# Second FFN layer as seven products of quarters, with operand sums on GpSimd

## The chip, the core and the metric

One Trainium2 chip, one core. The metric is the device time of one execution in microseconds (us); less is better. TensorE (PE) multiplies, VectorE (DVE), ScalarE (ACT) and GpSimd (POOL) work on tiles of 128 partitions, SyncE (SP) and two of the others issue DMAs. A tile of 128x512 float32 has 256 KB.

## What is computed

A trunk layer on 1024 latent rows and 128 prompt rows, 1152 in all, of width 1024. The change is in its last part, the FFN, and the final norm:

```python
h2 = rmsnorm(x, p['norm2_g']) * (1 + sc2) + sh2
a, b = jnp.split(h2 @ p['ffn_w1'], 2, axis=-1)
x = x + g2 * ((jax.nn.silu(a) * b) @ p['ffn_w2'])
...
y_prompt = rmsnorm(xp, final_norm_g)
y_sample = rmsnorm(xs, final_norm_g)
```

`ffn_w2` has 2816 rows, 22 tiles of 128, and 1024 columns. `sc2`, `sh2` and `g2` are one set for the latent rows and one for the prompt's. All is float32.

## The kernel before

A float32 product is made as three fast matmuls. Each operand is split into a high half (a cast on ScalarE) and a low half (source minus high, on VectorE), and `mm3` (L257 to L259) adds high x high, high x low and low x high in PSUM.

The first FFN layer (L1364 to L1366) runs over 22 pairs of weight tiles, one of `a` and one of `b`, on all 1152 rows. A pair is already made as seven products instead of eight: the weights' sums are made on GpSimd (`w_sum`, tile `ws`), three products ahead (`LEAD = 3`) of their matmuls, and split into `wf`. The pair's results go through `evac` into `st`, and `store` splits them into `hl` and writes both halves to DRAM (`hid_d`) from ScalarE's queue. Pair 0 is made apart, in four pieces, since the rows of `h2` come one by one.

The second layer runs in three passes over the inner dimension (tiles 0 to 5, 6 to 13, 14 to 21). In a pass, each of nine row tiles `i` takes its tile `hid` from DRAM and makes two halves of columns, each a chain of three matmuls per inner tile, `f<-w,hid` 128x512. The weights come as `w2r` and are split into `w` (`load_hl`, L1127 and L1128). After each half, VectorE multiplies the sum by the gate row `g2r` (L1570), and GpSimd adds it to `acc` (L1572), which holds `x`; in the last pass VectorE adds (L1574) and ScalarE squares (L1575), VectorE makes the mean (L1578, L1579), GpSimd the power (L280), VectorE the scaled result (L1584), and SP writes it out.

A scheduler sets the order of the instructions of each engine from the order of the code; each engine works its own list in order.

Of the kernel before, what the change touches and what calls it, by code (L numbers as in the profile page):

```python
# [84 lines left out]
def kernel(ctx: ExitStack, tc: tile.TileContext, A: dict, O: dict):  # L85
# [1252 lines left out]
    hid_d = [dp.tile([2, NT, P, b - a, P], F32, name=f"hid{a}_d") for a, b in PASSES]  # L1338

    def stages():  # L1340
        ts_ = [M("st", [P, 2, NCH, HALF]) for _ in range(2)]
        return [t[:, i] for t in ts_ for i in range(2)] + [M("st", [P, NCH, HALF])]
# [155 lines left out]
    def w2_place(j):  # L1498
        if j < 4 or 14 <= j < 18:
            t = zt("w2", [P, 2, D], 4, F32R)  # L1500
            return t[:, 0], t[:, 1]
        if 6 <= j < 12 or j == 21:
            i, n = divmod(j - 6, 3) if j < 12 else (0, 0)
            if n == 0:
                z[i] = wide["right"].tile([P, 3, 2, D], F32R, tag=f"xb{i}", name=nm("w2"), bufs=1)
            return z[i][:, n, 0], z[i][:, n, 1]
        return tuple(slot("w2", dt=F32R) for _ in range(2))

    def w2_load(j):
        if j in w2:  # L1510
            return
        w2[j] = load_hl(zt("w2r", [P, D], 4), *w2_place(j), A["w_ffn2"][j])

    def hid_load(n, i):
        if n == len(PASSES) or (n, i) in hid:
            return
        a, b = PASSES[n]
        t = zt("hid", [P, 2, 8, P], 3, F32R)
        for q in range(2):
            dma(f(t[:, q, :b - a]), hid_d[n][q, i])  # L1520
        hid[n, i] = t[:, 0], t[:, 1]

    order = [(j, i) for j in range(1, NF) for i in range(7)]
    pairs = {}
    for n, (j, i) in enumerate(order):
# [8 lines left out]
        if (j, i) == (NF - 1, 3):  # L1534
            xctx.__exit__(None, None, None)
            open_z()
            for i2 in range(6):
                if i2 < 3:
                    hid_load(0, i2)
                w2_load(i2)  # L1540
# [2 lines left out]
    g2rows, acc = [], []
    for n, (a, b) in enumerate(PASSES):
        for j in range(a, b):
            w2_load(j)
        for i in range(NT):
            for d in range(3):
                hid_load(n + (i + d) // NT, (i + d) % NT)
            h = hid.pop((n, i))  # L1550
            pts = [bank("f2", "m") for _ in range(2)]
            for j in range(a, b):
                for hf in range(2):
                    hs = slice(hf * 512, hf * 512 + 512)
                    last["f2"] = mm3(pts[hf], (h[0][:, j - a], h[1][:, j - a]), (w2[j][0][:, hs], w2[j][1][:, hs]), j == a, j == b - 1)
            if n == i == 0:
                for cnd in range(2):
                    g2rows.append(slot("g2r"))
                    bcast_row(g2rows[cnd], cnd, 5)
                fng = slot("fng")  # L1560
                dma(fng, A["final_g"].partition_broadcast(P))
            if n == 0:
                for i2 in ((0, 1) if i == 0 else (i + 1,) if i + 1 < NT else ()):
                    acc.append(M("acc", [P, D]) if i2 < 8 else slot("acc"))
                    nc.gpsimd.dma_start(acc[i2], x1_d[i2])
            st = small("nst", [P, 3])
            for hf in range(2):
                hs = slice(hf * 512, hf * 512 + 512)
                t = half_slot("fin")
                V.tensor_mul(t, pts[hf], g2rows[i == 8][:, hs])  # L1570
                if n < len(PASSES) - 1:
                    G.tensor_add(acc[i][:, hs], acc[i][:, hs], t)  # L1572
                else:
                    V.tensor_add(acc[i][:, hs], acc[i][:, hs], t)  # L1574
                    S.activation(t, acc[i][:, hs], AF.Square, accum_out=st[:, hf:hf + 1])  # L1575
            if n < len(PASSES) - 1:
                continue
# [165 lines left out]
```

## Time and profile before

| | us |
|---|---|
| median of 3 runs | 2148.88 (2144.29 to 2150.33) |
| the profiled execution | 2148.07 |
| its span, first to last instruction | 2145.9 |
| first layer after pair 0 | 1383.35 to 1856.6 |
| second layer, first to last start of a matmul | 1856.61 to 2137.03 |

The span lies within the execution; 2.2 us are around it. Of a row of the timeline, the bracket says how long the engine had stood idle, and what ended that. In groups by line, "xN | a, b" is the count, the busy time in us and the mean of one in ns.

### The profile page before, as it was taken

To read this page: it belongs to the slowest core of one execution; us is meant where nothing else is said; L and a number is where in the kernel's file an instruction comes from. 1 tells how busy PE (TensorE), PEld (TensorE's weight loads), DVE (VectorE), ACT (ScalarE), POOL (GpSimd) and SP (SyncE) were. 2 spreads that over 40 slices of the span, in tenths; PEclk is the share of its full clock that TensorE was granted. 3 is DMA by queue.
4 is the path that set the end of the run, shared out by engine and by line. 5 is a ranking of instruction groups with operands and counts; after the bars stand their busy time and mean duration, and the time that the engine had idled before them with its cause. 6 is when DMAs were issued, how large, how long until landed. Compare 5 with 4: busy or idle time off the path is not lost.

```text
span 2145.9 us, 31575 instructions
## 1 busy us (share of the span) xinstructions
PE 2070.2 (96%) x12400; PEld 1844.4 (86%) x12400; DVE 1158.8 (54%) x2123; ACT 727.2 (34%) x1320; POOL 406.5 (19%) x344
## 2 busy tenths in 40 slices
PE   6899999999999999999999998899999999999998
PEld 1558888998887799999999876799999999878886
DVE  4733499825443278998823266645445454432134
ACT  3734443445432533332223244423223232310011
POOL 1310020000001202232211234421221212042210
PEclk9999999999999999999999999899999999999999
DMA  8784552233242352242221342222423324764232
GB/s 289 219 278 142 190 185 97 66 105 129 75 146 83 120 193 89 95 133 67 88 69 58 128 157 108 91 84 84 126 84 111 99 88 122 255 236 151 84 137 88
DMA packets 174824, 276.20 MB, mean 129 GB/s; under 512 B 14834, under 2 KB 123987, under 8 KB 174548
## 3 DMA queue, kind: packets, MB, share of 16 engines
q1 hardware_dynamic: 120692, 238.80, 32.9%
q10 hardware_dynamic: 51392, 25.96, 4.4%
q0 software_dynamic: 2592, 9.44, 1.1%
q8 instruction: 97, 1.59, 0.3%
q14 instruction: 51, 0.42, 0.1%
HBM read 196.58 MB, written 77.56 MB: 128 GB/s over the span
## 4 chain that ended last, share of the span: by engine, by line
PE 86%; DVE 5%; DMA 4%; ACT 2%; issue 1%; SPq 1%; POOL 1%; ACTq 0%; DVEq 0%; POOLq 0%
PE gm L257 9%; PE gm L259 9%; PE gm L258 9%; PE f L1365 8%; PE f L1366 8%; PE f L1364 7%; PE f L259 4%; PE f L258 4%; PE f L257 4%; PE po L682 2%; PE ptr L672 2%; PE po L258 1%; PE po L259 1%; PE po L257 1%; PE wo L258 1%
## 5 line engine op out<-in xcount | busy, mean ns | idle before, releaser
L259 PE MATMUL gm<-hT_hi,wlo 128*128 128x384 f32 x1224 | 420.0, 343 | 2.7 <-DVE wlo L233 2.7
L257 PE MATMUL gm<-hT_hi,whi 128*128 128x384 f32 x1224 | 421.6, 344 | 0.7 <-ACT whi L232 0.4
L258 PE MATMUL gm<-hT_lo,whi 128*128 128x384 f32 x1224 | 417.3, 341 | 0.0
L259 PEld LDWEIGHTS gm<-hT_hi,wlo 128*128 128x128 f32 x1224 | 231.1, 189 | 11.5 <-issue 5.1
L257 PEld LDWEIGHTS gm<-hT_hi,whi 128*128 128x128 f32 x1224 | 231.0, 189 | 11.6 <-issue 7.5
L258 PEld LDWEIGHTS gm<-hT_lo,whi 128*128 128x128 f32 x1224 | 231.0, 189 | 5.7 <-issue 3.8
L1364 PE MATMUL f<-xa_hi,wf 128*128 128x288 f32 (+2 forms) x704 | 210.3, 301 | 9.2 <-ACT wf L1334 8.7
L1365 PE MATMUL f<-xa_lo,wf 128*128 128x288 f32 (+2 forms) x704 | 212.6, 303 | 2.1 <-DVE xa_lo L1301 1.9
L1366 PE MATMUL f<-xa_hi,wf 128*128 128x288 f32 (+2 forms) x704 | 210.9, 302 | 0.4 <-DVE wf L1335 0.4
L1173 POOL TENSOR_TENSOR mg<-mg,sg 128x384 f32<-128x384 f32 x72 | 97.3, 1352 | 364.8 <-DVE sg L1169 360.5
L257 PE MATMUL f<-w,hid 128*128 128x512 f32 x396 | 154.7, 394 | 4.2 <-DVE st L1388 2.1
L1365 PE MATMUL f<-xb,wf 128*128 128x288 f32 (+2 forms) x528 | 156.6, 297 | 0.6 <-DVE xb L1301 0.6
L1364 PE MATMUL f<-xb,wf 128*128 128x288 f32 (+2 forms) x528 | 156.9, 297 | 0.0
L1366 PE MATMUL f<-xb,wf 128*128 128x288 f32 (+2 forms) x528 | 156.4, 296 | 0.0
L258 PE MATMUL f<-w,hid 128*128 128x512 f32 x396 | 155.9, 394 | 0.2 <-DVE w L1128 0.2
L259 PE MATMUL f<-w,hid 128*128 128x512 f32 x396 | 155.3, 393 | 0.4 <-DMA hid<-hid_d 0.4
L1364 PEld LDWEIGHTS f<-xa_hi,wf 128*128 128x128 f32 x704 | 135.8, 194 | 10.9 <-ACT wf L1334 9.8
L1168 ACT ACTIVATE sg<-gm,vec 128x384 f32<-128x384 f32 x96 | 55.9, 582 | 243.0 <-PE gm L259 233.6
L1365 PEld LDWEIGHTS f<-xa_lo,wf 128*128 128x128 f32 x704 | 135.0, 192 | 3.7 <-DVE xa_lo L1301 3.4
L1366 PEld LDWEIGHTS f<-xa_hi,wf 128*128 128x128 f32 x704 | 134.5, 192 | 1.3 <-DVE wf L1335 1.2
L1570 DVE TENSOR_TENSOR fin<-f,g2r 128x512 f32<-128x512 f32 x54 | 37.1, 690 | 156.0 <-PE f L259 152.9
L1169 DVE SCALAR_TENSOR_TENSOR sg<-sg,po 128x384 f32<-128x384 f32 x96 | 52.6, 548 | 123.8 <-PE po L259 118.6
(359 smaller groups left out, 4196.7 us busy)
## 6 DMA issues: line engine op xcount, KB each, us to landing
hid_d<-hl ACTq DMA_DIRECT2D x44, 576.0 KB
adaw<-in_ada_w_dram SPq DMA_DIRECT2D x48, 512.0 KB
wraw<-in_w_ffn_dram SPq DMA_DIRECT2D x44, 512.0 KB
wraw<-in_w_gate_dram SPq DMA_DIRECT2D x32, 640.0 KB
hid<-hid_d SPq DMA_DIRECT2D x36, 512.0 KB
wraw<-in_w_o_dram SPq DMA_DIRECT2D x24, 512.0 KB
w2r<-in_w_ffn_dram SPq DMA_DIRECT2D x22, 512.0 KB
wraw<-in_w_in_dram SPq DMA_DIRECT2D x19, 512.0 KB
```

The costliest lines, as they stand in the source:

```text
L257: mm(out, ah, bh, start=start, stop=False)
L258: mm(out, ah, bl, start=False, stop=False)
L259: return mm(out, al, bh, start=False, stop=stop)
L672: tr(pt[:, k * P:(k + 1) * P], pe[:, (k0 + k) * P:(k0 + k + 1) * P], ident)
L682: mm(po[64 * j:64 * j + 64, :P], vtile(kt)[:, h * 64:(h + 1) * 64], pT[:, i, :], start=(i == 0), stop=(i == len(kts) - 1))
L1168: S.activation(sg, pg, AF.Tanh, bias=vc("gate_b", b * 8 + j), scale=0.5)
L1169: V.scalar_tensor_tensor(sg, sg, 1.0, po, op0=ALU.add, op1=ALU.mult)
L1173: G.tensor_add(merged[j][:, cs], merged[j][:, cs], sg)
L1364: mm(out, w[:, 0, ks], x[0], start=st, stop=False, skip_group_check=True)
L1365: mm(out, w[:, 0, ks], x[1], start=False, stop=False, skip_group_check=True)
L1366: mm(out, w[:, 1, ks], x[0], start=False, stop=sp_, skip_group_check=True)
L1570: V.tensor_mul(t, pts[hf], g2rows[i == 8][:, hs])
```

## The change

With the latent rows in two halves of 512 (four row tiles each), the inner dimension in two halves of 11 tiles (`KH`) and the columns in two halves of 512, the second layer becomes a product of 2x2 by 2x2 blocks, made as seven products of sums of blocks instead of eight of blocks. The prompt's 128 rows stay plain products, which are put into products 0, 4, 5 and 6, where a plain block of weights is at hand.

- `store` writes the pair's results unsplit: the prompt's part to `ask_d`, and, once both pairs `jj` and `jj + 11` are there, the blocks A11, A12, A22 and the sums S1 to S4, made on GpSimd (L1408), to `rows_d`. GpSimd issues these DMAs (L1397, L1400). The first layer's pairs run 0, 11, 1, 12 and so on.
- Each of 7 x 11 steps (product `n`, inner tile `jj`) is prepared three steps ahead: a load of rows `ar` (L1547) and of weights `br` (L1511) on SP, in products 1, 2, 3 and 5 a subtraction of weights on GpSimd (L1525, L1529, L1533), and the splits `ah` and `bh` (L1515 on ScalarE, L1516 on VectorE). In product 5 a further split `bx` serves the prompt.
- A step is 4 row tiles x 3 matmuls, and 3 more for the prompt in products 0, 4 and 5; in product 6 the prompt's stand after all steps in the code.
- `evacuate` copies and adds the PSUM sums into four tiles for each block of the result (`c11` and so on); gate, residual, squares and the multiplication by the norm's weights are made block by block.

```diff
-        def store(self):
-            hl = [M("hl", [P, NCH, 2, HALF], F32R) for _ in range(2)]
...
+            put("A11", a11)
+            put("A12", a12)
+            put("A22", a22)
...
+            for o, t, x, y, op in (("S1", s1, a21, a22, G.tensor_add), ("S2", s2, s1, a11, G.tensor_sub),
+                                   ("S3", s3, a11, a21, G.tensor_sub), ("S4", s4, a12, s2, G.tensor_sub)):
+                op(t, x, y)
+                put(o, t)
...
-    order = [(j, i) for j in range(1, NF) for i in range(7)]
+    def weights(jj):
+
+        b = w2_load(0, 0, jj)
+        yield b, None
+        for kh, nh in ((0, 1), (1, 1)):
+            x = w2_load(kh, nh, jj)
+            G.tensor_sub(x, x, b)
+            b = x
+            yield b, None
+        b21, x = w2_load(1, 0, jj), zt("br", [P, 512], 16)
+        G.tensor_sub(x, b21, b)
+        yield x, None
+        yield b21, None
+        b22, b12, x = w2_load(1, 1, jj), w2_load(0, 1, jj), zt("br", [P, 512], 16)
+        G.tensor_sub(x, b22, b12)
+        yield x, b12
+        yield b22, None
...
+        at = zt("ah", [P, 2, 512], 4, F32R)
+        ar = zt("ar", [P, 512], 4)
+        dma(ar, rows_d[SECOND[n], jj])
+        bt = zt("bh", [P, 2, 512], 4, F32R) if n < 6 or jj < 4 else slot("bh", [P, 2, 512], F32R)
+        ready[n, jj] = parts(at, ar), parts(bt, raw)
...
+    def residual(i, h, c):
...
+        V.tensor_mul(c, c, g2rows[i == 8][:, h * 512:h * 512 + 512])
+        G.tensor_add(c, c, x1)
...
+        residual(i, 0, c)
+        squares(i, 0, c)
+        G.tensor_mul(c, c, fng[:, :512])
+
+    def last_product(i, c, ps):
+        t = half_slot("lp")
+        V.tensor_mul(t, ps, g2rows[i == 8][:, 512:])
+        G.tensor_add(c, c, t)
+
+    def finish(i, c0, c1):
+
+        squares(i, 1, c1)
...
+        pow_mhalf(st[:, 3:4], st[:, 2:3])
...
+        V.scalar_tensor_tensor(c1, c1, st[:, 3:4], fng[:, 512:], op0=ALU.mult, op1=ALU.mult)
...
+        elif n == 2:
+            V.tensor_add(a["c21"], a["c11"], ps)
+            G.tensor_add(a["c12"], a["c12"], a["c21"])
...
+        elif n == 5:
+            V.tensor_add(a["c21"], a["c21"], ps)
+            V.tensor_add(a["c22"], a["c12"], ps)
+            residual(q, 1, a["c12"])
+            first_half(4 + q, a["c21"])
+            residual(4 + q, 1, a["c22"])
+            finish(4 + q, a["c21"], a["c22"])
+        else:
+            last_product(q, a["c12"], ps)
+            finish(q, a["c11"], a["c12"])
```

Up to the first rows of pair 0's results, every engine's list is the same as before. ScalarE at the end of pair 0, before: `st` is pair 0's result, `hl` its split, `wf` the split of the next pair's weights, `f` a PSUM bank.

```order
L1374 COPY st_12242<-f_2258_12479 128x192
L1378 ACTIVATE st_12243<-f_2258_12479 128x192
L1385 ACTIVATE st_12242<-st_12242 128x192
L1395 CAST hl_12577<-st_12244 128x3x192
L1395 CAST hl_12577<-st_12243 128x3x192
L1399 DMA hid_d<-hl_12577 128x9x128
L1399 DMA hid_d<-hl_12578 128x9x128
L1334 CAST wf_12589<-wraw_12585 128x512
L1374 COPY st_12613<-f_2275_12616 128x2x3x96
```

The same place of ScalarE after (`hid` takes the place of two of the `st`):

```order
L1376 COPY st_12318<-f_2258_12555 128x192
L1334 CAST wf_12665<-ws_12663 128x512
L1334 CAST wf_12668<-wraw_12654 128x512
L1334 CAST wf_12679<-ws_12661 128x512
L1334 CAST wf_12713<-ws_12711 128x512
L1380 ACTIVATE hid_12320<-f_2258_12555 128x192
L1334 CAST wf_12744<-ws_12742 128x512
L1334 CAST wf_12772<-wraw_12655 128x512
L1387 ACTIVATE st_12318<-st_12318 128x192
L1376 COPY st_12682<-f_2273_12685 128x2x3x96
```

The next pair's first cast (`wf_12589`) stood behind the `hl` rows and the DMAs; now that pair's casts stand between pair 0's rows (its first, `wf_12658`, 34 rows ahead of the first one shown).

VectorE before, for one row tile of the last pass, between its last matmul and its output (`fin` is the gated sum, `nst` the norm's small tile):

```order
L1570 TENSOR_TENSOR fin_18996<-f_2937_18945,g2r_17426 128x512
L1570 TENSOR_TENSOR fin_19000<-f_2938_18946,g2r_17426 128x512
L1574 TENSOR_TENSOR acc_17734<-acc_17734,fin_18996 128x512
L1574 TENSOR_TENSOR acc_17734<-acc_17734,fin_19000 128x512
L1578 TENSOR_TENSOR nst_18995<-nst_18995 128x1
L1579 TENSOR_SCALAR nst_18995<-nst_18995 128x1
L1584 SCALAR_TENSOR_TENSOR acc_17734<-acc_17734,nst_18995,fng_17430 128x512 x2
```

VectorE after, part of what stands between product 5's sums and the split of the rows of step (6,4), `ah_19327` (`c` a block of the result, `rows` the tile with the gate rows and the prompt's result):

```order
L1516 TENSOR_TENSOR ah_19307<-ar_19308,ah_19307 128x512
L1516 TENSOR_TENSOR bh_19310<-br_18881,bh_19310 128x512
L1603 TENSOR_TENSOR c_2817_18006<-c_2817_18006,rows_17442 128x512
L1603 TENSOR_TENSOR rows_17442<-rows_17442 128x512
L1603 TENSOR_TENSOR c_2767_17740<-c_2767_17740,rows_17442 128x512
L1603 TENSOR_TENSOR c_2988_18866<-c_2988_18866,rows_17442 128x512
L1516 TENSOR_TENSOR bh_19430<-br_19073,bh_19430 128x512
L1603 TENSOR_TENSOR c_2818_18007<-c_2818_18007,rows_17442 128x512
L1603 TENSOR_TENSOR c_2768_17741<-c_2768_17741,rows_17442 128x512
L1603 TENSOR_TENSOR c_2989_18867<-c_2989_18867,rows_17442 128x512
L1603 TENSOR_TENSOR c_2818_18007<-c_2818_18007,rows_17442 128x512
L1516 TENSOR_TENSOR ah_19327<-ar_19328,ah_19327 128x512
```

GpSimd at the same place, after (`x` the rows to which the gated sum is added):

```order
L1604 TENSOR_TENSOR c_2817_18006<-c_2817_18006,x_2990_18868 128x512
L1604 TENSOR_TENSOR c_2767_17740<-c_2767_17740,x_3064_19208 128x512
L1615 TENSOR_TENSOR c_2817_18006<-c_2817_18006,rows_17442 128x512
L1604 TENSOR_TENSOR c_2988_18866<-c_2988_18866,x_2990_18868 128x512
L1604 TENSOR_TENSOR c_2817_18006<-c_2817_18006,x_2991_18870 128x512
L1604 TENSOR_TENSOR c_2988_18866<-c_2988_18866,x_2991_18870 128x512
L1604 TENSOR_TENSOR c_2767_17740<-c_2767_17740,x_3068_19231 128x512
L1615 TENSOR_TENSOR c_2817_18006<-c_2817_18006,rows_17442 128x512
L1604 TENSOR_TENSOR c_2818_18007<-c_2818_18007,x_2992_18872 128x512
L1604 TENSOR_TENSOR c_2989_18867<-c_2989_18867,x_2992_18872 128x512
```

Each multiplication by the gate row on VectorE is followed by an addition on GpSimd, and four row tiles of the lower half pass here in full; 24 rows of VectorE run from the first sum of product 5 (L1651) to `ah_19327`, 12 of them shown.

## Rows read from the trace of the kernel before

**Rows 1.** The page: the span, and the chain that ended last by engine.

```profile
span 2145.9 us, 31575 instructions
...
PE 86%; DVE 5%; DMA 4%; ACT 2%; issue 1%; SPq 1%; POOL 1%; ACTq 0%; DVEq 0%; POOLq 0%
```

**Rows 2.** Groups by line and form of the stretch 1856 to 2146 us, the second layer: line, engine, operation, tiles and shapes, count | busy us, mean ns | idle us before them and what ended it.

```profile
L258 PE MATMUL f<-w,hid 128*128 128x512 f32 x396 | 155.9, 394 | 0.2 <-DVE w L1128 0.2
L259 PE MATMUL f<-w,hid 128*128 128x512 f32 x396 | 155.3, 393 | 0.4 <-DMA hid<-hid_d 0.4
L257 PE MATMUL f<-w,hid 128*128 128x512 f32 x396 | 154.7, 394 | 4.2 <-DVE st L1388 2.1 <-DMA hid<-hid_d 2.1
...
L1572 POOL TENSOR_TENSOR acc<-acc,fin 128x512 f32<-128x512 f32 x36 | 50.3, 1421 | 110.6 <-DVE fin L1570 110.6
...
L1584 DVE SCALAR_TENSOR_TENSOR acc<-acc,nst,fng 128x512 f32<-128x512 f32 x18 | 12.7, 749 | 6.3 <-POOL nst L280 6.3
```

**Rows 3.** Timeline of TensorE at the beginning and the end of the second layer: start us, us, engine, line, operation, tiles, shapes, count, [idle before <- what ended it].

```profile
1856.61 0.39 PE L257 MATMUL f<-w,hid 128*128 128x512 f32 x1
1857.19 0.50 PE L258 MATMUL f<-w,hid 128*128 128x512 f32 x1 [0.19 <-DVE w L1128]
...
1860.03 0.50 PE L257 MATMUL f<-w,hid 128*128 128x512 f32 x1 [2.10 <-DVE st L1388]
...
2137.03 0.40 PE L259 MATMUL f<-w,hid 128*128 128x512 f32 x1
```

**Rows 4.** Timelines of VectorE, GpSimd and SP at the end, same columns.

```profile
2136.76 1.39 DVE L1570 TENSOR_TENSOR fin<-f,g2r 128x512 f32<-128x512 f32 x2 [5.05 <-PE f L259]
2138.07 1.28 DVE L1574 TENSOR_TENSOR acc<-acc,fin 128x512 f32<-128x512 f32 x2
2140.29 0.16 DVE L1578 TENSOR_TENSOR nst<-nst 128x1 f32<-128x1 f32 x1 [0.94 <-ACT fin L1575]
2140.48 0.15 DVE L1579 TENSOR_SCALAR nst<-nst 128x1 f32<-128x1 f32 x1
2141.36 1.41 DVE L1584 SCALAR_TENSOR_TENSOR acc<-acc,nst,fng 128x512 f32<-128x512 f32 x2 [0.73 <-POOL nst L280]
...
2140.78 0.55 POOL L280 TENSOR_TENSOR nst<-nst,mhalf 128x1 f32<-128x1 f32 x1 [10.51 <-DVE nst L1579]
...
2142.14 0.99 SPq L1585 DMA_DIRECT2D out_y_prompt_dram<-acc  x2
```

**Rows 5.** Timelines of TensorE and ScalarE where pair 0 ends and the next pair begins.

```profile
1379.63 0.27 PE L1366 MATMUL f<-xb,wf 128*128 128x192 f32 x1
1383.35 0.40 PE L1364 MATMUL f<-xa_hi,wf 128*128 128x288 f32 x1 [3.45 <-ACT wf L1334]
...
1385.71 0.44 PE L1364 MATMUL f<-xa_hi,wf 128*128 128x288 f32 x1
1385.95 0.44 PE L1365 MATMUL f<-xa_lo,wf 128*128 128x288 f32 x1
...
1390.04 0.41 PE L1364 MATMUL f<-xa_hi,wf 128*128 128x288 f32 x1 [1.25 <-ACT wf L1334]
...
1380.72 0.67 ACT L1395 CAST hl<-st 128x576 fp32r<-128x576 f32 x1 [0.27 <-DVE st L1389]
1381.42 1.22 ACTq L1399 DMA_DIRECT2D hid_d<-hl  x2
1382.68 0.62 ACT L1334 CAST wf<-wraw 128x512 fp32r<-128x512 f32 x1 [1.29 <-DVE hl L1396]
```

**Rows 6.** The stretch 1440 to 1840 us of the first layer: busy us and count of each engine, granted clock, DMA share and rate; groups of GpSimd and ScalarE in it; and two neighbouring rows of VectorE's timeline.

```profile
1440.00:1840.00 400.00, 400.00 (x3008) 400.00 (x3007) 198.48 (x287) 124.10 (x216) 91.64 (x72) 1.00 0.33 97
...
L1316 POOL TENSOR_TENSOR ws<-ws,wraw 128x512 f32<-128x512 f32 x18 | 23.2, 1290 | 0.0
...
L1334 ACT CAST wf<-wraw 128x512 fp32r<-128x512 f32 x54 | 33.1, 613 | 0.0
...
1586.08 0.68 DVE L1335 TENSOR_TENSOR wf<-ws,wf 128x512 fp32r<-128x512 f32 x1
1586.68 0.68 DVE L1335 TENSOR_TENSOR wf<-wraw,wf 128x512 fp32r<-128x512 f32 x1
```

**Rows 7.** Timelines of VectorE and GpSimd in the second layer.

```profile
1885.36 0.69 DVE L1570 TENSOR_TENSOR fin<-f,g2r 128x512 f32<-128x512 f32 x1 [0.53 <-POOL acc L1572]
1885.97 4.13 DVE L1128 TENSOR_TENSOR w<-w2r,w 128x1024 fp32r<-128x1024 f32 x1
1890.36 1.23 DVE L1128 TENSOR_TENSOR w<-w2r,w 128x1024 fp32r<-128x1024 f32 x1 [0.27 <-ACT w L1127]
...
1896.67 1.57 DVE L1128 TENSOR_TENSOR w<-w2r,w 128x1024 fp32r<-128x1024 f32 x1 [0.18 <-ACT w L1127]
...
1881.54 7.47 POOL L1572 TENSOR_TENSOR acc<-acc,fin 128x512 f32<-128x512 f32 x6
1895.87 3.52 POOL L1572 TENSOR_TENSOR acc<-acc,fin 128x512 f32<-128x512 f32 x2 [6.86 <-DVE fin L1570]
```

**Rows 8.** The stretch 1860 to 1880 us, columns as in the first row of group 6: us, then busy us (count) of PE, PEld, DVE, ACT and POOL, granted clock of TensorE, DMA share, GB/s.

```profile
1860.00:1880.00 20.00, 19.97 (x87) 16.39 (x88) 12.41 (x13) 7.86 (x9) 2.65 (x5) 1.00 1.04 389
```

More of the change, by code (lines that the diff above doesn't have):

```diff
@@ L37 @@
 LEAD = 3
-PASSES = ((0, 6), (6, 14), (14, 22))
+KH = NF // 2
 VEC = {}
@@ L1336, in w_prepare @@
         split_ops[j, i] = t
[L1338 to L1342, printed above, removed]
+    ROWS = ("A11", "S1", "S2", "A22", "A12", "S3", "S4")
+    rows_d = {(o, jj): dp.tile([P, 512], F32, name=f"{o}_{jj}_d") for o in ROWS for jj in range(KH)}
+    ask_d = {h: dp.tile([P, KH, P], F32, name=f"ask{h}_d") for h in range(2)}
+    hids = {}
     class Pair:
@@ L1486 @@
     four = psum["left", "ctx"].__enter__()
-    z, w2, hid = {}, {}, {}
+    z = {}
     def open_z():
@@ L1496, in zt @@
         return z["pool"].tile(list(shape), dt, tag=tag, name=nm(tag), bufs=bufs)
[L1498 to L1521, printed above, removed]
-    order = [(j, i) for j in range(1, NF) for i in range(7)]
+    def w2_load(kh, nh, jj):
+        t = zt("br", [P, 512], 16)
+        dma(t, A["w_ffn2"][kh * KH + jj][:, nh * 512:nh * 512 + 512])
+        return t
@@ L1524 @@
+    steps = [(n, jj) for n in range(7) for jj in range(KH)]
+    order = [(j, i) for h in range(NF) for j in (h // 2 + h % 2 * KH,) if j for i in range(7)]
     pairs = {}
@@ L1536 @@
             open_z()
[L1537 to L1540, printed above, removed]
+            for st_ in steps[:LEAD]:
+                prepare(*st_)
     open_psum("J", "left", m=8)
[L1543 to L1577, printed above, removed]
[L1578 to L1585 removed]
@@ new lines, in product @@
+    def product(n, qs):
+        ps = {q: bank("f2", "m") for q in qs}
+        pp = bank("fp", "m") if n in PROMPT and n < 6 else None
+        for jj in range(KH):
+            s = steps.index((n, jj)) + LEAD
+            if s < len(steps) and steps[s] not in ready:
+                prepare(*steps[s])
+            (ah, al), b = ready[n, jj]
+            for q in qs:
+                ts_ = slice(q * P, q * P + P)
+                mm3(ps[q], (ah[:, ts_], al[:, ts_]), b, jj == 0, jj == KH - 1)
+            if pp is not None:
+                ask_part(n, pp, jj)
+        for q in qs:
+            evacuate(n, q, ps[q])
+        if pp is not None:
+            ask_evac(n, pp)
@@ new lines @@
+    for n in range(7):
+        if n in (0, 1, 2, 5):
+            place(("c11", "c12", "c21", None, None, "c22")[n])
+        if n == 1:
+            rows_loads()
+        if n == 5:
+            for i in range(4, 8):
+                t = slot("x1")
+                dma(t, x1_d[i])
+                x1s.update({(i, h): t[:, h * 512:h * 512 + 512] for h in range(2)})
+        product(n, range(4))
+    pp = bank("fp", "m")
+    for jj in range(KH):
+        ask_part(6, pp, jj)
+    ask_evac(6, pp)
```

107 lines of the change are left out of this document (89 added, 18 removed).

## Prediction

> **What bounds the kernel now.** I read the page first: TensorE is 86% of the chain that ended last [rows 1]. The second FFN layer is the stretch from the first to the last matmul of `f<-w,hid`, 1856.61 to 2137.03 us [rows 3]. The groups by line and form [rows 2] give 3 x 396 = 1188 matmuls there, and 4.2 + 0.2 + 0.4 = 4.8 us of idle TensorE ahead of them, so one matmul costs (280.42 - 4.8) / 1187 = 0.2322 us. This stage is bound by the number of its matmuls. So is the first layer: TensorE is busy 400 of 400 us between 1440 and 1840, 400 / 3008 = 0.133 us a matmul [rows 6]. Three places have TensorE waiting: the seam of pair 0 and the next pair [rows 5], the seam of the two layers [rows 3], and the tail, in which the last rows go through VectorE, ScalarE, GpSimd, VectorE and out, 2145.9 - 2137.4 = 8.5 us [rows 4].
>
> **One thing that the rows show of VectorE beside GpSimd.** At 1885.97 a VectorE subtraction of 128x1024 with both operands in SBUF took 4.13 us; the same one at 1890.36 took 1.23 [rows 7]. GpSimd was then in a run of six additions, 1881.54 to 1889.01 (7.47 / 6 = 1.25 each); the slow one ends 1.1 us behind that run. At 1895.87 two GpSimd additions took 3.52 instead of 2.5, with a VectorE subtraction of 1.57 between them. But the VectorE multiplication at 1885.36, with one operand in PSUM, took 0.69 beside the same run. So a VectorE instruction with two SBUF operands and a GpSimd instruction run one after the other, and I count both on one line.
>
> **The change, step by step.**
>
> *Matmuls.* 7 products x 11 steps x 4 row tiles x 3, and 11 x 4 x 3 for the prompt: 924 + 132 = 1056. 132 fewer x 0.2322 = **-30.6**. The stage's own waits go with its old order: **-4.8**.
>
> *First layer.* Two ScalarE casts, two VectorE subtractions and two DMAs a pair leave. GpSimd gets, for two pairs, four sums and nine DMA issues beside its eight weight sums: 12 x 1.29 + 9 x about 0.5 (ScalarE's two issues took 1.22, [rows 5]; I put the same or less) = 20 of 2 x 168 x 0.133 = 44.7 us. With VectorE's two-operand work of some 13 us (14 splits of 0.60 each, their spacing in [rows 6], and the last steps of the gate) the line holds 28 of 44.7: hidden, **0**. If it were not, 11 double pairs would pay the excess each.
>
> *Seam of pair 0.* TensorE stood 3.45 + 1.25 us [rows 5], and the matmuls between ran 0.24 apart instead of 0.133 for about 14 of them (1.5 us): 6.2 lost. ScalarE did pair 0's `hl` casts and 1.22 us of DMA issues ahead of the first `wf` cast. Now that cast stands far ahead and the `hl` rows are gone. What is late next is VectorE's last evacuation of pair 0, whose PSUM bank the next pair takes; the same kind of wait at the layers' seam is 2.10 [rows 3], the old wait 3.45. I take 2.8 left: **-3.4** (0 to -5).
>
> *Seam of the layers.* The wait for the last pair's bank stays: 2.1. Then the four sums of the last double pair, 4 x 1.25 = 5 us in a run on GpSimd, stand beside the splits of steps 3 to 6 on VectorE, while TensorE has 48 matmuls and part of the prompt's (11 to 14 us) in hand. Between 0 and 5 us; I take 3. Together **+5**.
>
> *Steps.* A step is 12 matmuls, 2.79 us. ScalarE: two casts of 0.61 [rows 6]. The line: two splits (1.20) and in products 1, 2, 3 and 5 one GpSimd subtraction (1.25), 2.45 of 2.79: covered, with 0.34 spare. In product 3 the four GpSimd additions of product 2 come on top, 5 us against 11 x 0.34 = 3.7 of spare, and behind them a third split a step for product 5; three steps are prepared ahead, but VectorE works in order. From 0 to 7; I take **+3.5**.
>
> *Between products 5 and 6.* VectorE's rows from the first evacuation of product 5 to the low half of (6,4) are 24, of 0.60: 14.4 us. Ten GpSimd rows fall in them, 12.5 us. On one line that is 26.9, less some 2 that lie beside the eight adds from PSUM: 25 us. TensorE has 82 matmuls before it needs that low half, 82 x 0.2322 = 19.0. It waits 6, and by the same count about 4 over the next three steps: **+10** (0 if the two engines overlap: 14.4 is under 19). A wait of 3.45 was followed by matmuls at half speed, 1.5 us [rows 5]: **+1.5**.
>
> *Tail.* The last product's tile 0 ends 20 matmuls, 4.6 us, before TensorE. From it five tiles follow each other, each with GpSimd add 1.25, VectorE 0.16 + 0.15, GpSimd power 0.55, VectorE scale 0.75 [rows 2, 4] on the line: 2.86 each. The scale of the last ends -4.6 + 0.7 + 5 x 2.86 = 10.4 us behind TensorE; before it was 2142.77 - 2137.43 = 5.3. **+5.1** (+3 if only GpSimd and the chain of one tile count).
>
> Sum: -30.6 - 4.8 - 3.4 + 5 + 3.5 + 10 + 1.5 + 5.1 = -13.7. The profiled run took 2148.07 us (span 2145.9 and 2.2 around it), near the median 2148.88: **2134.4 us**.
>
> The Trainium skill bears on this at two places. "SBUF — State Buffer", section "Who interferes with whom", has the two engines share one port pair as an exclusive lock, and whichever starts first holds it for its instruction; a waiting VectorE instruction would then lose at most the rest of one GpSimd instruction, 1.25. The row of 4.13 us shows it passed over by more than two in a run. By the page the run of four sums at the layers' seam would cost at most 1.25 instead of 3, and the sum would be 2132.6. "GPSIMD Engine Reference", section 4.1, speaks against the change: it puts elementwise sums on VectorE, GpSimd being about half as fast. The rows agree on the speed (1.29 against 0.68, [rows 6]); but moving the 44 + 44 sums would not shorten TensorE's stage, since the line above carries both, so its price here is only what the line already has.
>
> **Rivals.**
> (a) *The engines overlap after all*: then 3, 3.5, 10, 1.5 and 2 of the tail go, and the time is 2148.1 - 33.7 = 2114. Rows of 0.68 beside GpSimd would speak for it, [rows 7] against. 0.12.
> (b) *Loads pace the steps; slower.* Each step loads 2 x 256 KB in 2.79 us, 188 GB/s, into four buffers a kind; a buffer's round (load, cast, split, 12 matmuls) may take 4 x 2.79 = 11.2 us. From 12.0 us on, a step is 3.0, and 66 steps lose 0.2 each, which eats the 13.7; at 14 us the loss is 66 x 0.7 = 46 and the time 2180. For it: 389 GB/s with all queues full at the stage's start [rows 8], where before too a transfer ended last (2.1, [rows 2]). Against: after that the stage needs half of this. 0.09.
> (c) *The gain is eaten, no more*: waits at the seam and in product 5 (three splits, 1.86 + 1.25 on the line, and fifteen rows for the evacuation of product 4) of another 8 to 20 us: 2142 to 2155. 0.14.
> That the change does nothing to the count of matmuls is excluded by the code.
>
> **How the numbers follow.** The forecast, 2121 to 2142, has 0.65, with its terms' bounds: the seam terms +-3, the steps +-3.5, product 6 from 5 to 15. The range takes half of (a) and half of (c): 2117 to 2147. Within 0.3% (6.4 us, about what a measurement of this kernel can tell from no change) of 2148.9 is (c); (b) is slower; faster is 0.65 + 0.12.
>
> **What would show it.** 1056 matmuls 0.232 apart; `ah` and `bh` splits on VectorE of 1.5 to 4 us instead of 0.6, each beside GpSimd; TensorE waiting for VectorE `ah` some 19 us into the last product, and 0 at product boundaries; a tail of 13 to 14 us. Wrong would be: splits at 0.6 throughout, or TensorE's waits naming the loads of `ar` or `br`, or GpSimd the releaser in the first layer.

## The result, and the profile after

| | before | after |
|---|---|---|
| median of 4 runs | 2146.59 us (2142.14 to 2150.33) | 2124.56 us (2119.2 to 2128.58) |
| ratio | | 0.9897, 95% interval 0.9865 to 0.9928 |
| the profiled execution, its span | 2148.07, 2145.95 | 2125.52, 2123.74 |
| up to the first matmul of the first FFN layer (code unchanged) | 1316.16 | 1314.33 |
| from there to the first matmul of the second layer | 540.45 | 536.62 |
| second layer, first to last start of a matmul | 280.42 | 258.23 |
| from the end of the last matmul (0.4 us after its start) to the end | 8.52 | 14.17 |

The change takes 22 us off; 13.7 were forecast. By the profiles the second layer gains 22.2 us and the first 3.8, the tail pays 5.7 back, and 1.8 lie ahead of the first layer, on unchanged code.

The stretch ahead of the first FFN layer ran between 1310.6 and 1316.9 us in the profiles below, on unchanged code. So the experiments are compared by stage, and by time only where the kernels ran beside each other in several rounds.

What TensorE waited for in the second layer after the change (view of waits, 1845 to 2145 us: total us, times, longest):

```profile
PE f L259 <- DVE ah L1516: 4.9, 2, 4.4
PE fp L257 <- DVE c L1646: 2.6, 1, 2.6
PE fp L259 <- DVE ask L1582: 2.1, 1, 2.1
PE f L257 <- DVE st L1390: 2.0, 1, 2.0
PE f L258 <- DVE bh L1516: 1.3, 2, 0.7
```

Together 12.9 us. VectorE is the releaser in every row, no load and no GpSimd instruction. Without them the matmuls start (258.23 - 12.9) / 1055 = 0.2325 us apart in the mean, where the prediction had 0.2322 [rows 2, 3]; two things, of which the prediction had 1.5 us of one, cancel in that number, and they are told below.

Groups of the same stage, 1850 to 2124 us, answering [rows 2]:

```profile
L1516 DVE TENSOR_TENSOR ah<-ar,ah 128x512 fp32r<-128x512 f32 x75 | 73.2, 978 | 34.9 <-ACT ah L1515 33.4 <-DMA br<-in_w_ffn_dram 1.5
L1516 DVE TENSOR_TENSOR bh<-br,bh 128x512 fp32r<-128x512 f32 x74 | 71.2, 968 | 1.3 <-ACT bh L1515 1.1
L1525 POOL TENSOR_TENSOR br<-br,br 128x512 f32<-128x512 f32 x22 | 36.1, 1667 | 9.9 <-DMA br<-in_w_ffn_dram 7.5 <-ACT ah L1515 2.4
L1604 POOL TENSOR_TENSOR c<-c,x 128x512 f32<-128x512 f32 x16 | 26.5, 1664 | 19.3 <-DVE c L1603 19.3
...
L1651 DVE TENSOR_TENSOR c<-c,f 128x512 f32<-128x512 f32 x4 | 2.7, 676 | 0.0
```

The splits take 0.97 us in the mean; the same shape takes 0.68 in [rows 6]. GpSimd's operations are stretched too, 1.67 against 1.25 to 1.29 in [rows 6, 7]. VectorE's additions with an operand in PSUM (L1651) stay at 0.68.

### The profile page after: what moved, and what is told of

The parts are those of the page before. It is cut to its first block, busy times and chain, and to the rows that moved or that the text cites. A ratio compares the mean times of both kernels' runs of the same rounds, so it can differ in the third digit from the quotient of the medians.

```text
span 2123.7 us, 32145 instructions
## 1 busy us (share of the span) xinstructions
PE 2040.1 (96%) x12268; PEld 1821.2 (86%) x12268; DVE 1282.2 (60%) x2187; ACT 785.0 (37%) x1440; POOL 583.5 (27%) x522
## 4 chain that ended last, share of the span: by engine, by line
PE 70%; DVE 9%; DMA 3%; issue 3%; ACT 2%; POOL 1%; SPq 0%; DVEq 0%; POOLq 0%; ACTq 0%
PE gm L257 8%; PE f L1368 8%; PE f L1366 8%; PE f L1367 7%; PE gm L259 7%; PE gm L258 7%; PE po L682 2%; PE f L259 2%; PE f L257 2%; PE f L258 2%; PE ptr L672 2%; PE wo L258 1%; PE po L258 1%; PE po L257 1%; PE wo L259 1%
## 5 line engine op out<-in xcount | busy, mean ns | idle before, releaser
L257 PEld LDWEIGHTS gm<-hT_hi,whi 128*128 128x128 f32 x1224 | 230.0, 188 | 13.2 <-issue 7.5
L259 PE MATMUL f<-bh,ah 128*128 128x512 f32 x308 | 121.2, 396 | 4.9 <-DVE ah L1516 4.9
L258 PE MATMUL f<-bh,ah 128*128 128x512 f32 x308 | 121.1, 393 | 1.3 <-DVE bh L1516 1.3
L257 PE MATMUL f<-bh,ah 128*128 128x512 f32 x308 | 119.4, 393 | 2.0 <-DVE st L1390 2.0
L1335 DVE TENSOR_TENSOR wf<-ws,wf 128x512 fp32r<-128x512 f32 x88 | 104.0, 1212 | 5.9 <-ACT wf L1334 5.9
```

The costliest lines, as they stand in the source:

```text
L257: mm(out, ah, bh, start=start, stop=False)
L258: mm(out, ah, bl, start=False, stop=False)
L259: return mm(out, al, bh, start=False, stop=stop)
L1335: V.tensor_sub(t[:, 1], src, f(t[:, 0]))
```

## What the profile shows between products 5 and 6

VectorE, then GpSimd, from the middle of product 5's evacuation to the row for which TensorE waits, and TensorE itself (timeline columns as in [rows 3]):

```profile
2063.08 0.68 DVE L1651 TENSOR_TENSOR c<-c,f 128x512 f32<-128x512 f32 x1
...
2078.41 6.83 DVE L1603 TENSOR_TENSOR c<-c,rows 128x512 f32<-128x512 f32 x4
2085.16 1.75 DVE L1516 TENSOR_TENSOR ah<-ar,ah 128x512 fp32r<-128x512 f32 x1
...
2077.97 3.37 POOL L1604 TENSOR_TENSOR c<-c,x 128x512 f32<-128x512 f32 x2 [1.23 <-DVE c L1603]
2081.30 1.72 POOL L1615 TENSOR_TENSOR c<-c,rows 128x512 f32<-128x512 f32 x1
2082.98 6.74 POOL L1604 TENSOR_TENSOR c<-c,x 128x512 f32<-128x512 f32 x4
...
2086.96 2.08 PE L259 MATMUL f<-bh,ah 128*128 128x512 f32 x4 [4.36 <-DVE ah L1516]
```

Four VectorE rows take 6.83 and four GpSimd rows 6.74: the two engines alternate, one instruction each per 1.70 us. This is the "one line" of the prediction, but cheaper: 1.25 + 0.60 = 1.85 was counted. From the first evacuation (2063.08) to the end of the awaited split (2086.91) are 23.8 us, where 25 were counted. TensorE ran dry at 2086.96 - 4.36 = 2082.6, 19.5 us after that first evacuation (19.0 counted), and waited 4.36.

## Experiments

The theory is the line: a VectorE instruction with two operands in SBUF and a GpSimd instruction take turns, and what waits is read off the sum of both. Its first rival is that the engines overlap and something else, such as the loads, makes the waits; the second is that each wait has a cause of its own. Except where medians are named, times are those of single profiled executions.

| kernel | time, us | second layer | its waits | at the lower clock | behind its last matmul | span |
|---|---|---|---|---|---|---|
| after | 2125.52 | 258.23 | 12.9 | 6.8 | 14.17 | 2123.74 |
| e1_sub_twice | 2141.85 | 274.92 | 20.8 | 20.5 | 14.16 | 2140.08 |
| e2_no_sub | 2120.14 | 251.06 | 7.0 | 6.8 | 14.18 | 2118.18 |
| e3_resid_on_vector | 2124.98 | 255.64 | 10.5 | 6.8 | 16.66 | 2123.20 |
| e5_changed_again | 2129.66 | 260.67 | 15.2 | 6.8 | 14.14 | 2127.89 |
| e6_last_add_on_vector | 2124.73 | 261.15 | 14.4 | 10.2 | 11.97 | 2122.97 |
| e7_line_relieved | 2123.46 | 253.28 | 9.7 | 3.4 | 13.30 | 2121.67 |
| e8_fifteen_br | 2125.1 | 260.21 | 13.2 | 10.2 | 14.15 | 2123.19 |
| e9_relieved_fifteen | 2110.63 | 249.60 | 5.5 | 3.4 | 13.29 | 2108.86 |
| e10_relieved_again | 2121.15 | 253.70 | 8.5 | 6.8 | 13.31 | 2119.36 |

The changed kernel, twice, differs by 2.4 us in its second layer; less than that between two single profiles tells nothing. "Its waits" are the second layer's idle times of TensorE, "at the lower clock" the time in it with a granted clock of 0.50, the lower of TensorE's two levels (1.2 GHz); in the kernel before, that layer ran at 1.00 throughout. Such stretches stand behind waits of TensorE, but not behind each (behind the one for `c`, in e3 and e10, not in the changed kernel). Taking the waits and half of the time at the lower clock off the second layer leaves 241.6 to 242.4 us in every row but e1 (243.9) and e2 (240.6): what the experiments change is the waits and the clock that comes with them.

### More and less work for GpSimd

Every subtraction of weights on GpSimd made twice:

```diff
             G.tensor_sub(x, x, b)
+            G.tensor_sub(x, x, b)
...
         G.tensor_sub(x, b21, b)
+        G.tensor_sub(x, x, b)
...
         G.tensor_sub(x, b22, b12)
+        G.tensor_sub(x, x, b12)
```

> The changed kernel with each of the 44 subtractions of weights on GpSimd in the second layer made twice (the result is no longer the reference's). Theory 1, one line for VectorE's two-operand splits and GpSimd: a step of products 1 to 3 asks for 2 x 1.25 + 2 x 0.60 = 3.7 us of the line and TensorE needs 2.79, so the second layer becomes about 20 us longer (from 258 to some 275 to 290), with TensorE waiting for VectorE's bh or ah in products 1 to 3. Theory 2, the engines overlap and VectorE is only late by its own number of rows: GpSimd has 2.5 of 2.79 us a step, nothing changes (258 +- 3). Theory 3, the loads of ar and br are what is late: nothing changes, and waits name the loads.

Measured: the second layer takes 274.92 us, 16.7 more. The waits of TensorE there, the row of 1924 to 1955 us (the end of product 1 and product 2; columns as in [rows 8]) and the group of one split:

```profile
PE f L258 <- DVE bh L1516: 7.1, 15, 1.4
PE f L259 <- DVE ah L1516: 7.0, 2, 6.8
...
1924.00:1955.00 31.00, 27.57 (x111) 19.88 (x110) 31.00 (x20) 13.38 (x24) 29.87 (x18) 1.00 0.39 121
...
L1516 DVE TENSOR_TENSOR ah<-ar,ah 128x512 fp32r<-128x512 f32 x77 | 104.7, 1364 | 6.1 <-ACT ah L1515 5.8
```

In that stretch VectorE shows as busy for 31.0 of 31 us with 20 instructions and GpSimd for 29.87 with 18: no loads are late, the two fill the line, and TensorE now waits within products, 15 times. Two subtractions a step are 2.5 and two splits 1.2: 3.7 us a step by the count, over the 2.79 of its matmuls. Of the 44 x 1.25 = 55 us more on the line, 7.9 became waits of TensorE (20.8 instead of 12.9); most of the other 8.8 us is the clock, which behind these waits was 0.50 for 20.5 instead of 6.8 us.

The subtractions taken out:

```diff
-            G.tensor_sub(x, x, b)
...
-        b21, x = w2_load(1, 0, jj), zt("br", [P, 512], 16)
-        G.tensor_sub(x, b21, b)
-        yield x, None
+        b21 = w2_load(1, 0, jj)
...
-        b22, b12, x = w2_load(1, 1, jj), w2_load(0, 1, jj), zt("br", [P, 512], 16)
-        G.tensor_sub(x, b22, b12)
-        yield x, b12
+        yield b21, None
+        b22, b12 = w2_load(1, 1, jj), w2_load(0, 1, jj)
+        yield b22, b12
```

> The changed kernel without the 44 subtractions of weights on GpSimd in the second layer: raw blocks of weights go into the products, and the same splits and matmuls (the result is not the reference's). Theory 1 (one line): the splits of products 1 to 3 fall from a mean near 0.98 to 0.7 us, the three waits at the change from product 3 to 4 (0.7, 0.6, 2.6 us, one of them put down to VectorE's c of L1646) go, the wait for ah in product 6 stays, since no subtraction falls there: second layer about 4 us shorter, 254. Theory 2 (overlap; VectorE's own rows): all waits stay, 258. Theory 3 (loads): all waits stay or grow.

Measured: 251.06 us, 7.2 less. A split now takes 0.80 in the mean, and beside the wait for the last pair's bank (2.7) one is left:

```profile
PE f L259 <- DVE ah L1516: 4.3, 2, 3.9
...
L1516 DVE TENSOR_TENSOR ah<-ar,ah 128x512 fp32r<-128x512 f32 x77 | 61.7, 802 | 62.1 <-ACT ah L1515 61.8
```

The waits between the products and for `ask` are gone. The wait in product 6 stays at its size: there GpSimd adds the residual, and no weights are subtracted. This run also has 22 fewer tiles of `br` to keep, so it does not settle by itself what made the wait between products 3 and 4; that is taken up below.

### Product 6: the residual on VectorE

```diff
-        G.tensor_add(c, c, x1)
+        V.tensor_add(c, c, x1)
...
-        G.tensor_mul(c, c, fng[:, :512])
+        V.tensor_mul(c, c, fng[:, :512])
```

> The changed kernel with the additions of x (L1604) and the multiplications by the norm's weights (L1615) on VectorE instead of GpSimd. Theory 1 (one line): between product 5 and the low half of (6,4) the line holds some 34 rows of 0.60 = 20.4 us instead of 24; the wait of 4.4 us falls to about 1 or goes, and 0.5 behind it goes; second layer about 5 to 8 us shorter (250 to 254). Theory 2 (overlap): VectorE's own rows grow from 24 to 34, from 14.4 to 20.4 us against TensorE's 19: the wait does not shrink, the stage stays or grows by 1 to 2 us. The tail: the same add of the last product is still on GpSimd, 13 to 16 us.

Measured: there is no wait for `ah` at all, though VectorE now has 30 instead of 24 rows up to the split of step (6,4). VectorE, from the first evacuation to the pair of splits of which the first is that one:

```profile
2066.23 0.68 DVE L1651 TENSOR_TENSOR c<-c,f 128x512 f32<-128x512 f32 x1
...
2081.25 1.89 DVE L1603 TENSOR_TENSOR c<-c,rows 128x512 f32<-128x512 f32 x3
...
2083.66 1.29 DVE L1516 TENSOR_TENSOR ah<-ar,ah 128x512 fp32r<-128x512 f32 x2
```

The split ends at 2084.3, 18.1 us behind the first evacuation, 30 rows of 0.60; in the changed kernel it was 23.8 with 24 rows. More work on one engine is faster than less on it beside the other, which excludes overlap. The time is within 0.6 us of the changed kernel's all the same: the second layer is 2.6 us shorter (5.0 shorter than in e5, the changed kernel's second profile; 5 to 8 were expected) and the tail 2.5 longer. The first evacuation of product 6 (L1619) came at 2104.48, 1.7 us ahead of the last matmul's start, in the changed kernel at 2105.00, 4.2 us ahead; from there to the end it is 18.7 us in both. So the end hangs on when the first row tile of product 6 is complete, not on the last matmul, and that moved by 0.5 us only: the scheduler has set the prompt's matmuls, the last 11 in the changed kernel, ahead of the last ones of the row tiles.

### The tail

```diff
     def last_product(i, c, ps):
...
-        G.tensor_add(c, c, t)
+        V.tensor_add(c, c, t)
```

> The changed kernel with one thing moved: the addition of the last product (L1620, five of 1.25 us on GpSimd) is made by VectorE (0.60). Theory 1 (the five tiles of the tail pass one after the other over VectorE and GpSimd, 2.74 us each): a tile takes 2.1 to 2.3, the tail behind the last matmul falls from 14.2 to 12 or 12.5; the stage of matmuls stays, 258. Theory 2 (the tail is the chain of the last tile alone, and the four ahead of it are hidden): only 1.25 - 0.60 is won, 13.5.

The changed kernel's tail first (VectorE; L1632 makes a tile's last half):

```profile
2109.18 0.75 DVE L1632 SCALAR_TENSOR_TENSOR c<-c,fst,rows 128x512 f32<-128x512 f32 x1
2109.84 1.22 DVE L1626 TENSOR_TENSOR fst<-fst 128x1 f32<-128x1 f32 x1
...
2111.91 0.75 DVE L1632 SCALAR_TENSOR_TENSOR c<-c,fst,rows 128x512 f32<-128x512 f32 x1
```

And with the addition on VectorE:

```profile
2110.10 0.75 DVE L1632 SCALAR_TENSOR_TENSOR c<-c,fst,rows 128x512 f32<-128x512 f32 x1
2112.25 0.75 DVE L1632 SCALAR_TENSOR_TENSOR c<-c,fst,rows 128x512 f32<-128x512 f32 x1
```

A tile follows the one before by 2.73 us in the changed kernel (2.86 forecast) and by 2.15 in the experiment; the tail goes from 14.17 to 11.97 us, and the second layer (261.15) is that of e5 (260.67). Even the 128x1 operation of L1626 takes 1.22 instead of 0.15 us beside GpSimd's addition. The rest of the tail is the chain of the last tiles and the output.

### The seam of pair 0, in the kernel before

Here the kernel before is changed: pair 0's splits and DMAs come after the next weights in the code.

```diff
     first_pair(2, 3)
-    pair0.store()
     for i in range(LEAD):
         w_prepare(1, i)
+    pair0.store()
```

> The kernel before with one thing moved: pair 0's store (its hl casts, splits and two DMA issues on ScalarE's queue) stands behind the preparation of the next pair's first three weights in the code. Theory 1 (ScalarE's list was what made TensorE wait there): the wait of 3.45 us falls to 1 to 2.5 and the one of 1.25 may go; the first layer, from its first matmul to the second layer's first, becomes 2 to 4 us shorter (540.4 to 537 or 538). Theory 2 (the raw weights of the next pair land late): the waits stay, 540 +- 1. The second layer as before, 280.

Measured: 2144.85 us (single), where the kernel before took 2146.81 on that chip. The first layer took 538.47 instead of 540.45 us. The wait of 3.45 for `wf` [rows 5] became one of 0.45 for VectorE's evacuation:

```profile
1375.00 0.53 PE L1365 MATMUL f<-xa_lo,wf 128*128 128x192 f32 x1 [1.47 <-DVE xa_lo L1301]
1383.74 0.40 PE L1364 MATMUL f<-xa_hi,wf 128*128 128x288 f32 x1 [0.45 <-DVE st L1388]
```

So the old wait was that of the casts behind pair 0's store, as the prediction had it, and this part of the gain needs no quarters. A wait for `xa_lo` grew from 0.57 to 1.47 in exchange. The changed kernel shows the same two rows, 1.46 and 1.25, and won 3.8 us of the first layer, but 1.5 in its second profile (538.96): pair 0 itself varies between 64.8 and 68.8 us in the ten profiles on the changed kernel's code. What lies behind it, from the next pair's first matmul to the second layer, does not: 473.26 us before, 470.15 to 470.44 in those ten, 469.53 here.

### The line relieved at both places

```diff
-        G.tensor_add(c, c, x1)
+        V.tensor_add(c, c, x1)
...
-        G.tensor_mul(c, c, fng[:, :512])
+        V.tensor_mul(c, c, fng[:, :512])
...
-        G.tensor_add(c, c, t)
+        V.tensor_add(c, c, t)
...
-        S.dma_start(out[:, :512], c0)
+        dma(out[:, :512], c0)
...
-        for jj in range(KH):
+        late = 3 if n == 6 else 0
+        for jj in range(KH - late):
...
+            for jj in range(KH - late, KH):
+                (ah, al), b = ready[n, jj]
+                ts_ = slice(q * P, q * P + P)
+                mm3(ps[q], (ah[:, ts_], al[:, ts_]), b, jj == 0, jj == KH - 1)
```

The last edit finishes product 6 by row tiles in its last three steps, so that the first row tile is complete earlier. It ran beside the changed kernel. What each of these edits is worth in this kernel was not tried.

> The changed kernel as it is, timed beside the next ones on one chip: 0.990 of the kernel before (2146 to 2125), second layer 258 us from the first to the last start of a matmul, 14.2 us behind the last matmul.

> What the runs so far point to: the changed kernel with all sums behind the products (x, the norm's weights, the last product) on VectorE, so that GpSimd keeps the sums of operands only; the last three steps of product 6 row tile by row tile; and all outputs issued by SP. Theory 1 (one line): no wait for ah in product 6 (4.9 us less), a tail of 12 to 13.5, second layer 250 to 255: 2115 to 2119 us, 0.986 of the kernel before, faster than the changed kernel by 5 to 9 us. Theory 2 (what leaves GpSimd comes back as VectorE's own work): 2125, as the run with only x and the norm's weights on VectorE, whose tail took back what the stage won.

Measured over 4 runs each: the changed kernel 2127.26 us (ratio to before 0.9898, 0.988 to 0.9916), the relieved one 2119.2 (0.9865, 0.9847 to 0.9883); 8.1 us by the medians. VectorE in product 6 now runs its rows 0.60 apart, `ah` among them:

```profile
2083.07 1.89 DVE L1603 TENSOR_TENSOR c<-c,rows 128x512 f32<-128x512 f32 x3
2084.88 0.69 DVE L1604 TENSOR_TENSOR c<-c,x 128x512 f32<-128x512 f32 x1
2085.48 1.29 DVE L1516 TENSOR_TENSOR ah<-ar,ah 128x512 fp32r<-128x512 f32 x2
```

The wait for `ah` is gone; those for `ask` (3.7 us) and `c` (2.7 us) are as in e5. The second layer took 253.28 against 260.67 us, the tail 13.30 against 14.14.

### The wait between products 3 and 4

The prediction put this wait on the line too. It stands in e3 and e7 too, but these leave GpSimd's work of products 2 and 3 as it is and could not test that. ScalarE and VectorE show something else there, in the changed kernel:

```profile
1976.87 0.62 ACT L1515 CAST bx<-br 128x512 fp32r<-128x512 f32 x1 [7.28 <-DMA br<-in_w_ffn_dram]
...
1977.53 1.29 DVE L1516 TENSOR_TENSOR bx<-br,bx 128x512 fp32r<-128x512 f32 x1 [5.51 <-ACT bx L1515]
...
1990.47 1.26 DVE L1516 TENSOR_TENSOR bx<-br,bx 128x512 fp32r<-128x512 f32 x1 [2.79 <-ACT bx L1515]
1991.66 0.68 DVE L1646 TENSOR_TENSOR c<-c,f 128x512 f32<-128x512 f32 x1
```

`bx`, the prompt's split for product 5, stands on both engines ahead of splits of product 4, and its load is late; VectorE waits for it 5.5, 2.7 and 2.8 us; the splits of `bh` for which TensorE waits (0.6 and 0.7 us) stand behind the first two, and the evacuation (L1646) that frees TensorE's bank behind the third. With 15 instead of 16 buffers for `br` the scheduler sets the first ones of `bx` one step of two splits later (not two, as the expectation below has it), and orders SP's loads otherwise. ScalarE's list, as a difference to 16:

```
-L1515 CAST bx_18739<-br_18727 128x512
 L1515 CAST ah_18428<-ar_18429 128x512
 L1515 CAST bh_18431<-br_18426 128x512
+L1515 CAST bx_18739<-br_18727 128x512
 L1515 CAST ah_18452<-ar_18453 128x512
 L1515 CAST bh_18455<-br_18450 128x512
-L1515 CAST bx_18771<-br_18759 128x512
```

The edit, at its three places, on the changed kernel (e8) and on the relieved one (e9):

```diff
-        t = zt("br", [P, 512], 16)
+        t = zt("br", [P, 512], 15)
```

> The changed kernel with 15 instead of 16 buffers for `br`. Nothing is computed otherwise; the scheduler, which knows one buffer less, puts the prompt's split `bx` behind the splits of two steps of product 4 instead of ahead of them, on ScalarE and on VectorE. Open is the wait of TensorE where product 3 ends and product 4 begins (c L1646 2.6 and bh L1516 1.3 in the changed kernel, and 2.7 and 1.0 in the kernel with the line relieved, e7, in which the other waits on the line went). Theory 'order': ScalarE there waits for the load of `br` that the first `bx` needs (7.3 us), and VectorE's splits of product 4 stand behind it; with `bx` later both waits of TensorE go, 3 to 4 us of the second layer (258.2 to about 254.5), and the wait for `ah` in product 6 stays at 4.9. Theory 'line': the GpSimd additions of product 2 and subtractions of product 3 are late; the waits stay at 3 to 4 us, since nothing on the line has changed.

> The kernel with the line relieved (e7: residual additions and the last additions on VectorE, the last three steps of product 6 ordered by row tiles) and 15 buffers for `br`. If the waits between products 3 and 4 come from the place of `bx`, they go (c L1646 2.7 and bh 1.0) and the kernel is 2.5 to 4 us faster than e7 beside it, 2115 to 2118 us; if they come from the line, it is within 1 us of e7.

> The kernel of e7 once more, unchanged, on the same chip as e8 and e9, so that one buffer less is the only difference to e9: 2119 us by e7's own measurement, and the same waits of TensorE as there (ask 3.7, c 2.7, st 2.4, bh 1.0).

Waits of TensorE in the second layer, e8 first, then e9:

```profile
PE f L259 <- DVE ah L1516: 6.4, 2, 6.2
PE f L258 <- DVE bh L1516: 3.8, 5, 1.5
```

```profile
PE f L257 <- DVE st L1390: 2.4, 1, 2.4
PE fp L259 <- DVE ask L1582: 2.1, 1, 2.1
PE f L258 <- DVE bh L1516: 1.0, 1, 1.0
```

The wait for `c` is gone in both; e10, the relieved kernel with 16, has it at 2.3. So it hangs on the place of `bx`. That the loads came in time is not the reason: in e9 VectorE still waits 4.9, 3.4 and 2.1 us for the first three of `bx`, with three evacuations (L1646) now ahead of the third. The wait for `bh` stays, against both expectations (1.0 in e9): it stands behind the second `bx`.

But only e9 keeps the gain. Its median is 2113.16 us against 2120.53 of e10 beside it (means 7.2 apart, with an interval of 3.4 to either side), and its second layer is 4.1 us shorter: waits of 5.5 instead of 8.5 us, and the lower clock for 3.4 instead of 6.8 (e10 has a second such stretch behind the wait for `c`). Between the profiled executions, a further 6.1 us lie ahead of the first FFN layer, 1310.6 against 1316.7 us, where the code is the same, and are no gain to count on.

In e8 the second layer was no shorter (260.21, between e5 and the changed kernel's first profile), against the expectation of 254.5: `bh` grew from 1.3 to 3.8 and `ah` from 4.9 to 6.4 us. Counted from the stage's first matmul, product 5 begins at 173.6 us instead of 175.9, but product 6 at 213.1 instead of 213.6: a wait for `bh` of 1.5 us in product 5 took most of the gain. Product 6 lost 2.5 more, with a wait for `ah` of 6.2 instead of 4.4 us and the lower clock for 6.8 instead of 3.4 us behind it. That a wait taken away ahead of a full line is given back at it fits both runs, but was not tried by itself.

e9 beats both kernels: ratio to before 0.9827 (0.981 to 0.9843). What held the load of `br` for `bx` shows in part: in the changed kernel, from 1945 to 1995 us, SP waits 11.6 us for GpSimd's subtractions (L1529) and 5.8 us for `bx` before it issues loads of `br`, and GpSimd stands idle 1.1 to 5.2 us before each of its last six subtractions there, until a load lands. So the line is not full where `bx` is late. Whether the stretch ahead of it, in which the two engines alternate (1958 to 1965 us), set this off is open; e2, without the subtractions, has none of these waits. More buffers were not tried.

## Why the prediction was right, and where its sizes were off

The direction held, the time lies in the range, and the line is what made the waits in product 6 and the tail as forecast; in products 3 and 4 the cause was another than the one named, and that the matmuls' time came out is luck. The sum was 8.5 us short of the profile's gain (13.7 against 22.2 between the spans), and it goes as follows.

| step | forecast | measured |
|---|---|---|
| 132 fewer matmuls (counted, at the old 0.2322), and the old waits | -35.4 | -35.4 |
| clock behind the wait in product 6; spacing of matmuls | +1.5 | +0.4 |
| seam of pair 0 (whole first layer) | -3.4 | -3.8 (-1.5 in e5) |
| seam of the layers | +5 | 2.0 + 2.1 = +4.1 |
| steps, products 3 and 4 | +3.5 | 2.6 + 1.3 = +3.9 |
| product 6: `ah` | +10 | +4.9 |
| tail | +5.1 | +5.7 |
| ahead of the first FFN layer | 0 | -1.8 |

**Matmuls: the number right, its parts not.** TensorE at full clock and busy throughout, 50 us before and 50 us after (columns as in [rows 8]):

```profile
1950.00:2000.00 50.00, 50.00 (x216) 40.26 (x215) 5.53 (x8) 0.00 (x0) 11.07 (x9) 1.00 0.28 100
```

```profile
1900.00:1950.00 50.00, 50.00 (x222) 41.40 (x221) 30.72 (x37) 23.12 (x42) 15.80 (x11) 1.00 0.46 138
```

222 matmuls instead of 216: undisturbed, they start 0.227 us apart now (the median of the starts) and 0.232 before. That is 1055 x 0.005 = 5.3 us to the good that was not forecast. What made them closer was not tried. It was used up at the waits: 258.23 - 12.9 - 1055 x 0.227 = 5.8 us are matmuls that stand wider, most of them behind the waits of the seam (2.0 us, to 1853.84) and of product 6 (4.4 us, to 2086.96). There the granted clock was 0.50 (columns as in [rows 8]):

```profile
1854.37:1857.79 3.42, 3.42 (x9) 2.67 (x8) 0.21 (x1) 0.10 (x1) 2.79 (x4) 0.50 1.05 395
2086.48:2089.89 3.41, 2.93 (x7) 2.35 (x8) 3.41 (x3) 1.58 (x5) 3.24 (x2) 0.50 0.30 77
```

Matmuls start 0.43 us apart in them; half of these 6.8 us, 3.4, is about what the clock cost; the rest of the 5.8 was not traced. That the 5.3 and the 5.8 cancel is luck. The prediction charged this once, 1.5 us behind the longest wait (there the granted clock was 0.71 from 2086.9 to 2092 us), and forgot the seam.

**First layer and tail: right.** The first layer was hidden although the line showed there too: between 1440 and 1840 us TensorE is busy all the time (columns as in [rows 8]; then VectorE's splits of the weights' sums):

```profile
1440.00:1840.00 400.00, 400.00 (x3003) 400.00 (x3002) 209.92 (x251) 100.30 (x179) 175.54 (x185) 1.00 0.26 91
...
L1335 DVE TENSOR_TENSOR wf<-ws,wf 128x512 fp32r<-128x512 f32 x72 | 88.4, 1258 | 0.0
```

The splits of `ws` go to 1.26 us each, GpSimd from 91.64 [rows 6] to 175.54 us, and TensorE does not wait.

**Product 6: the mis-sized step.** "A wait of 6, and by the same count about 4 over the next three steps" measured 4.4 and 0.5. The 6 was the count's 25 - 19.0; the trace has 23.8 - 19.5. Two things failed. The price of an alternating pair is 1.70, not 1.85. And the "4 over the next three steps" carried the count's deficit on, though behind that split the next two of `ah` follow within 5.7 us (2.37 for both at 2090.20), while TensorE, which has waited once, needs them 2.79 us later each. These 5.1 us are most of the miss.

**Seam of the layers: size about right, mechanism right.** VectorE beside the sums of the last double pair, GpSimd, and TensorE:

```profile
1858.34 7.48 DVE L1516 TENSOR_TENSOR ah<-ar,ah 128x512 fp32r<-128x512 f32 x2 [3.77 <-ACT ah L1515]
1865.75 2.69 DVE L1582 TENSOR_TENSOR ask<-rows,ask 128x1408 fp32r<-128x1408 f32 x1
...
1858.54 0.56 POOL L1400 DMA_DIRECT2D S_d<-rs  x1
1859.12 1.30 POOL L1408 TENSOR_TENSOR rs<-rs,hid 128x512 f32<-128x512 f32 x1
1860.37 1.31 POOL L1525 TENSOR_TENSOR br<-br,br 128x512 f32<-128x512 f32 x1
...
1862.72 1.30 POOL L1408 TENSOR_TENSOR rs<-hid,rs 128x512 f32<-128x512 f32 x1
...
1868.49 0.50 PE L259 MATMUL fp<-bh,ask 128*128 128x512 f32 x1 [2.11 <-DVE ask L1582]
```

Two splits took 7.48 us beside the sums, and `ask`, next on VectorE, made TensorE wait 2.1 us. That wait varies, from none (e2, e8) to 3.7 (e3, e5, e7). "SBUF — State Buffer" of the Trainium skill, section "Who interferes with whom", says that a VectorE operation with two SBUF inputs contends with a GpSimd operation that reads SBUF, and that one with at most one SBUF input, outside the two-port modes, does not; the rows here agree (means of 0.97 to 1.26 us for the splits, 0.68 for L1651). Its rule that the lock goes to whoever issues first, for the whole instruction (written there of the two-port modes), bounds a delay by the rest of one GpSimd instruction only if the waiting engine is next. Here it was not: the first of the two splits took 4.43 us, and two GpSimd operations (1859.12 and 1860.37) began and ended within it.

**Steps of products 3 and 4: right number, wrong cause.** The +3.5 was argued from the line; 3.9 was measured, all of it behind a `bx` whose load is late (for `c`, 2.6, by rows and experiment; for `bh`, 1.3, by the rows alone). The prediction named the "third split a step" and "VectorE works in order", but as load on the line, not as a wait ahead of the others; that the number came out is luck. Whether the line has a share in the late loads is open.

**Rivals.** The engines do not overlap (e3, e1), although the time came out between the forecast and that rival's 2114. The loads do not pace the steps: no TensorE wait names one, though a late one stands behind `bx`. ("Four buffers a kind" holds for `ar`; `br` has 16.) Waits of 8 to 20 us more did not come. What the prediction said a trace would show, it shows, but for two things: the splits' times lie between 0.68 and 4.43 us with a mean of 0.97, where 1.5 to 4 was written; and 3.9 us of waits stand around the change from product 3 to 4, where the boundaries were to have none.

## What to carry to other kernels

Count VectorE's instructions with two SBUF operands and GpSimd's on one line, at 1.70 us for an alternating pair of 128x512 float32. Where that line takes longer than TensorE's work beside it, moving an elementwise operation from GpSimd to VectorE is cheaper even though VectorE gets more to do; where it does not, as in the first layer, the blocking is free. Price a wait once, let it push back everything that is needed behind it, and look at the granted clock behind it before putting a difference down to waits alone. Take a wait's cause from the list of the engine that releases it: the same engine was released late here once by the line and once by an instruction ahead of its turn.
